# Product-sums of the adaLN modulation, moved in part from VectorE to GpSimd and ScalarE

## Chip, cores and metric

One core of a Trainium2 chip (trn2). The metric is the device time of one execution in microseconds, lower is better. The engines are named as in the profile: PE (TensorE, the matmuls), PEld (its weight loads), DVE (VectorE), ACT (ScalarE), POOL (GpSimd) and SP (SyncE, which here issues nearly all DMAs). Each engine works through its own queue in order; semaphores hold an instruction until its inputs are there and its output tile is free.

## What is computed

A decoder block of 512 positions and 1024 channels, in float32: a state-space mixer and a pooling mixer side by side, merged by gates, and then an MLP. Both halves begin with a norm that is shifted, scaled and gated by a vector `c` (adaLN). All that matters here is the modulation:

```python
mod = (jax.nn.silu(c) @ w_ada[i] + b_ada[i])[:, None, :]
shift_m, scale_m, gate_m, shift_f, scale_f, gate_f = jnp.split(mod, N_MOD, axis=-1)
h = rmsnorm(x, norm_mix_w[i]) * (1.0 + scale_m) + shift_m
x = x + gate_m * hybrid_mixer(h, ...)
h = rmsnorm(x, norm_mlp_w[i]) * (1.0 + scale_f) + shift_f
x = x + gate_f * (jnp.square(jax.nn.relu(h @ w_up[i])) @ w_down[i])
return rmsnorm(x, norm_final_w)
```

`mod` has 6 x 1024 values, each the sum over 1024 products of a row of the transposed `w_ada` with silu(c).

## The kernel before

Channels lie on the 128 partitions, positions on the free axis, so x and h are eight tiles of 128x512. float32 products are made exact enough by splitting each operand into a rounded high part and a low rest (ACT makes the high part, DVE subtracts it) and running three matmuls for each pair. A unit is one 128x1024 block of weights: a DMA into one of four RAW tiles, a cast on ACT (line 144), a subtraction on DVE (line 145), the parts in two of eight HL tiles, and 24 matmuls (lines 154 to 156).

**The modulation.** `mod` is a tile of 128x48; column j is the j-th block of 128 channels (0 to 7 shift, 8 to 15 scale, 16 to 23 gate, 24 to 47 the same for the MLP). `cbc` holds silu(c) on every partition. `ada(j)` loads the j-th 128x1024 block of the transposed `w_ada` (512 KB) and makes the column with one DVE instruction, which multiplies, sums along the free axis and adds the bias (line 170); a very short instruction then reads the sum out.

**The first stage** is written under `manual_schedule`: every engine takes its instructions in the order of the program. After `ada(8)` and `ada(0)`, eight steps k follow. Each loads and splits its starting weights (line 273 on ACT, line 277 on DVE, a 32-column cast on POOL, line 278), makes two columns of `mod` (line 170), the scale on ACT (line 264), the normalised and scaled x on DVE (line 302), its shifted high part on ACT (line 303) and the low part on DVE (line 305), and 18 matmuls over six units of projections (line 315) with two narrow ones for dt (line 309). The tiles of adaT lie in eight EARLY tiles, which are tiles of later stages.

**After it** the order of each engine's queue is set by a scheduler: the program order is the priority, `high_priority` goes ahead of it, and an instruction can be put earlier than its place in the program when its inputs and its tile are free. `issue_after(ins)` holds instructions behind `ins` on its engine. Four groups of the state-space mixer follow (`ssd_group`), with other units between their steps as fillers. Each group uses four 128x1024 tiles m (from three MT tiles) for the decay matrix; the last readers of m are the matmuls of line 520. Beside the fourth group run the pooling units (`pool_in`, with the running sums of line 600, the first of them on POOL and the others on DVE, line 604 and the split of line 125) and `pool_mix`.

Then come three loops of eight units: gates with `wgate[8 + j]`, each with `ada(16 + j)`; the pooling branch with `wbp[j]` and `ada(24 + j)`; the gates of the other branch with `wgate[j]` (lines 696 to 701) and `ada(32 + j)`, held behind the split of that step. The output loop with `wout[j]` has the residual (line 728), its square (line 735) and sum (line 736), and the last eight columns, two in a step from j = 2 on. In all these the tile of adaT is one of the four RAW tiles, which the weights use too. The MLP follows and is not touched.

Of the kernel before, what the change touches and what calls it, by code (L numbers as in the profile page):

```python
# [7 lines left out]
F32 = mybir.dt.float32  # L8
F32R = mybir.dt.float32r
AF = mybir.ActivationFunctionType  # L10
ALU = mybir.AluOpType

P = 128
# [29 lines left out]
class Slots:  # L43
# [13 lines left out]
    def put(self, *ts):  # L57
        for t in ts:
            self.free.append(self.owner.pop(id(t))[0])


def block_kernel(tc, xp, crow, arow, par, adaT, wstart, wz, wx, wpool_in, wgate, wpw, wbs, wbp, wout, wup, wdn, out):
    nc = tc.nc
    act, dve, pool, pe, sp = nc.scalar, nc.vector, nc.gpsimd, nc.tensor, nc.sync

    with (
# [23 lines left out]
        MT = Slots(lambda i, dt: D(NRAW + NHL + i, dt).rearrange("p (h k) -> p h k", h=HG), 3)  # L90
# [7 lines left out]
        def col(name, j=0, n=1, rows=P):  # L98
            a = COLS[name] + j
            return par_t[:rows, a:a + n]  # L100
# [5 lines left out]
        mod = sb.tile([P, 48], F32, name="mod")  # L106
        amod = sb.tile([P, 16], F32, name="amod")
        tri = sb.tile([P, P], F32, name="tri")
        zeros = sb.tile([P, NC], F32, name="zeros")
        ea = sb.tile([P, NH], F32, name="ea")  # L110
        dtk = sb.tile([P, NC, NH], F32, name="dtk")
        ncs = sb.tile([P, NC, NH], F32, name="ncs")
        cd = [sb.tile([P, NC, HG], F32, name=f"cd{i}") for i in range(2)]
        dec = [sb.tile([P, NC, HG], F32, name=f"dec{i}") for i in range(2)]
        cbc = D(NRAW + NHL + 3, F32)
# [3 lines left out]
        done = [None]  # L119
# [46 lines left out]
        def ada(j, at=RAW):  # L166

            r = at.get()
            sp.dma_start(r, adaT[j])
            dve.tensor_tensor_reduce(r, r, cbc, 1.0, col("b_ada", j), ALU.mult, ALU.add, mod[:, j:j + 1])  # L170
            at.put(r)

        def column_sums(ps, sqs, c0, c1, opened=False):

# [41 lines left out]
        EARLY = Slots(lambda i, dt: early[i // 2][:, 2 * (i % 2):2 * (i % 2) + 2, :].rearrange("p a b -> p (a b)"), 8)  # L216
        with tc.manual_schedule():
            raw0 = RAW.get()
            crow_t = raw0[:1]
            act.dma_start(crow_t, crow)  # L220
            mt = [MT.get() for _ in range(3)]
            xs1 = HL.get()
            xpair = [m.rearrange("p h k -> p (h k)") for m in mt] + [xs1]
            xs0 = [xpair[k // 2][:, k % 2 * T:k % 2 * T + T] for k in range(8)]
            for i in range(4):
                sp.dma_start(xpair[i], xp[i])
            sp.dma_start(par_t, par)
            warm(12)
            wide = HL.get()
            dve.memset(wide, 0.0)  # L230
            act.activation(wide[:1], crow_t, AF.Silu)
            cps = [PU.get(), PU.get()]
            for i in range(2):
                pe.matmul(cps[i], ones, wide[:, i * T:(i + 1) * T], start=True, stop=True)
            HL.put(wide)
            ps = PU.get()
            sq = [HL.get() for _ in range(4)]

            def halves(i):
                dve.tensor_tensor(sq[i][:, :T], sq[i][:, :T], sq[i][:, T:], ALU.add)  # L240

            def sums(i):
                pe.matmul(ps, ones, sq[i][:, :T], start=i == 1, stop=i == 3)

            for i in range(3):
                act.activation(sq[i], xpair[i], AF.Square)
                halves(i)
                if i == 1:
                    dve.tensor_tensor(sq[1][:, :T], sq[1][:, :T], sq[0][:, :T], ALU.add)
            act.copy(cbc[:, :T], cps[0])  # L250
            act.activation(sq[3][:, :T], xpair[3][:, :T], AF.Square)
            act.copy(cbc[:, T:], cps[1])
            act.preload_act_table_set("natural_log_exp_and_others")
            dve.tensor_tensor(sq[3][:, T:], xpair[3][:, T:], xpair[3][:, T:], ALU.mult)
            halves(3)
            for i in range(1, 4):
                sums(i)
            warm(5)
            PU.put(*cps)
            RAW.put(raw0)  # L260
            HL.put(*sq)

            def scale(k):
                act.activation(amod[:, k:k + 1], mod[:, 8 + k:9 + k], AF.Identity,
                               bias=col("nmix", k), scale=col("nmix", k))

            W0 = 6 * P + NH

            def begin(k):

                r, hi, lo = RAW.get(), HL.get(F32R), HL.get(F32R)
                sp.dma_start(r[:, :W0], wstart[k])
                act.copy(hi[:, :W0], r[:, :W0])
                return r, hi, lo

            def end(r, hi, lo):
                dve.tensor_tensor(lo[:, :W0], r[:, :W0], hi[:, :W0].bitcast(F32), ALU.subtract)
                pool.tensor_copy(hi[:, W0:W0 + NH], lo[:, W0 - NH:W0].bitcast(F32))
                RAW.put(r)
                HL.put(hi, lo)  # L280
                return [(hi[:, o:o + n], lo[:, o:o + n]) for o, n in [(6 * P, 2 * NH)] + [(o, P) for o in range(0, 6 * P, P)]]

            h = []
            ada(8, EARLY)
            R = S.get()
            act.activation(R, ps, AF.Ln, bias=eps_t, scale=1.0 / DM)
            act.activation(R, R, AF.Exp, scale=-0.5)
            PU.put(ps)
            ada(0, EARLY)
            scale(0)  # L290
            first = [PS.get() for _ in range(8 - NPU)] + [PU.get() for _ in range(NPU - 1)]
            for k in range(8):
                hi, lo = S.get(F32R), S.get(F32R)
                h.append((hi, lo))
                t = S.get()
                shift = mod[:, k:k + 1]
                w = begin(k)
                if k:
                    ada(8 + k, EARLY)
                    scale(k)  # L300
                    ada(k, EARLY)
                dve.scalar_tensor_tensor(t, xs0[k], amod[:, k:k + 1], R, ALU.mult, ALU.mult)
                act.activation(hi, t, AF.Identity, bias=shift)  # L303
                w = end(*w)
                dve.scalar_tensor_tensor(lo, t, shift, hi.bitcast(F32), ALU.add, ALU.subtract)
                S.put(t)
                def dt_unit():
                    for i in range(2):
                        pe.matmul(first[0][:2 * NH], w[0][0], h[k][i], start=k == 0 and i == 0, stop=k == 7 and i == 1)

                for i in range(3):
                    if k == 7 and i == 2:
                        dt_unit()
                    for u in range(1, 7):
                        pe.matmul(first[u], w[u][i // 2], h[k][i % 2], start=k == 0 and i == 0, stop=k == 7 and i == 2)  # L315
                if k < 7:
                    dt_unit()
            sp.dma_start(ea, arow[0:1, :].broadcast_to([P, NH]))
            act.activation(ea, ea, AF.Exp)
# [349 lines left out]
        for j in range(8):  # L669
            gp = F.get()  # L670
            ps = unit(wgate[8 + j], h)
            behind(act.activation(gp, ps, AF.Sigmoid))
            PU.put(ps)
            merged.append(gp)
            if j == 1:
                for _ in rest:
                    pass
                later.append(SZ.get())
                F.free += range(12, 16)
                PU.free += PS.free  # L680
            if j == 3:
                for i in range(4):
                    bs(3, i)()
                pool_mix(1)()
            ada(16 + j)
        for j in range(8):
            ps = unit(wbp[j], pout)
            dve.tensor_tensor(merged[j], merged[j], ps, ALU.mult)
            PU.put(ps)
            ada(24 + j)  # L690
        free(pout)
        mg = []
        for j in range(8):
            gs = F.get()
            ps = unit(wgate[j], h)
            last = act.activation(gs, ps, AF.Sigmoid)
            PU.put(ps)
            dve.tensor_tensor(gs, gs, acc[j], ALU.mult)
            dve.tensor_tensor(gs, gs, merged[j], ALU.add)
            S.put(acc[j])  # L700
            F.put(merged[j])
            mg.append(split(gs))
            F.put(gs)
            with tc.issue_after(done[0].ins):
                ada(32 + j)
        free(h)
        with tc.issue_after(last.ins):
            table = act.preload_act_table_set("natural_log_exp_and_others")
# [42 lines left out]
        for j in range(5):  # L751
            ps = unit(wout[j], mg)
            residual(ps, j, 16)
            PU.put(ps)
            ada(40 + j)
            if j > 1:
                ada(43 + j)
        for k in range(8):
            dve.tensor_scalar(
                amod[:, 8 + k:9 + k], mod[:, 32 + k:33 + k], 1.0, col("nmlp", k), ALU.add, ALU.mult)  # L760
# [405 lines left out]
```

## Time and profile before

| what | value |
|---|---|
| median of 3 runs | 972.45 us (971.51 to 973.26) |
| profiled execution, its own time | 972.32 us |
| span of the profiled execution | 970.6 us |
| busy: PE, DVE, ACT, POOL | 953.3, 658.7, 532.0, 62.8 us |
| product-sums in the first stage, 128x1024 (line 170) | 16, 1.27 to 1.28 us each |
| product-sums later (line 170) | 32, 1.28 us each, from 382.4 to 598.9 us |
| granted clock of PE | 0.996 |

The span runs from the first to the last instruction of the program; the own time has in addition what lies around it. The ends of matmuls are modelled, so that a busy PE isn't a PE at its peak. A row of a timeline has the start, the duration, the engine, the line, the operation, the output and inputs, and in brackets how long the engine had been idle and what ended that. Durations of neighbours on DVE overlap by some 0.07 us; from start to start is what an instruction takes of the queue. "SPq L169" is the issue of a DMA on SP. In a list of instructions of one line stand the shortest, median and longest duration in ns.

### The profile page before, as it was taken

How to read it: one execution, taken by the hardware profiler on the slowest of the kernel's cores; microseconds unless marked ns; L12 is line 12 of the kernel's file. 1: busy time of each engine (PE TensorE's matmuls, PEld its weight loads, DVE VectorE, ACT ScalarE, POOL GpSimd, SP SyncE). 2: the span in 40 equal slices, each digit the busy share in tenths (PEclk: the TensorE clock that was granted, in tenths of full speed). 3: DMA queues.
4: the chain of work that ended last, by engine and by line, in shares of the span. 5: the costliest groups of instructions: out<-in, count | busy, mean ns of one | idle time of the engine just before them, and what ended most of it. 6: DMA issues, size and time to landing. Idle time of an engine off the chain costs nothing.

```text
span 970.6 us, 13204 instructions
## 1 busy us (share of the span) xinstructions
PE 953.3 (98%) x5119; PEld 802.8 (83%) x5119; DVE 658.7 (68%) x965; ACT 532.0 (55%) x830; POOL 62.8 (6%) x71
## 2 busy tenths in 40 slices
PE   8999999999999999999999999999999999999996
PEld 4777778888878878788888878998899889889986
DVE  7996958475776586978533887895557556764633
ACT  6488988579538932562321433684157236425732
POOL 0101120130012012200000000000000000000000
PEclk9999999999999999999999999999999999999998
DMA  9747433442454244327733588441144225204002
GB/s 372 270 142 198 130 99 104 114 126 70 120 142 119 87 120 116 128 88 256 237 87 107 177 279 251 152 153 57 64 138 133 65 70 171 86 35 151 24 1 87
DMA packets 61761, 129.22 MB, mean 133 GB/s; under 512 B 4673, under 2 KB 29377, under 8 KB 61698
## 3 DMA queue, kind: packets, MB, share of 16 engines
q1 hardware_dynamic: 61696, 128.38, 41.5%
q8 instruction: 40, 0.66, 0.3%
q14 instruction: 23, 0.19, 0.1%
q10 hardware_dynamic: 2, 0.00, 0.0%
HBM read 126.13 MB, written 2.23 MB: 132 GB/s over the span
## 4 chain that ended last, share of the span: by engine, by line
PE 88%; DVE 5%; DMA 3%; ACT 2%; issue 1%; POOL 0%; DVEq 0%; SPq 0%; ACTq 0%; POOLq 0%
PE ps L154 22%; PE ps L155 22%; PE ps L156 22%; PE ps L864 12%; PE ps L315 3%; PE ps L520 1%; PE ps L504 1%; PE ps L500 1%; DMA d<-wout 1%; DVE d L170 1%; PE ps L476 1%; DMA d<-adaT 1%; DMA d<-cs_d 1%; DMA d<-wup 0%; DMA d<-xp 0%
## 5 line engine op out<-in xcount | busy, mean ns | idle before, releaser
L154 PE MATMUL ps<-s,d 128*128 128x512 f32 (+1 forms) x1088 | 416.0, 383 | 3.2 <-ACT d L144 1.1
L155 PE MATMUL ps<-s,d 128*128 128x512 f32 (+1 forms) x1088 | 411.7, 379 | 0.0
L156 PE MATMUL ps<-s,d 128*128 128x512 f32 (+1 forms) x1088 | 411.4, 379 | 0.0
L154 PEld LDWEIGHTS ps<-s,d 128*128 128x128 f32 x1088 | 204.3, 188 | 45.4 <-issue 2.4
L156 PEld LDWEIGHTS ps<-s,d 128*128 128x128 f32 x1088 | 204.5, 188 | 38.8 <-DVE d L145 0.3
L155 PEld LDWEIGHTS ps<-s,d 128*128 128x128 f32 x1088 | 204.8, 188 | 37.4 <-DVE s L125 0.2
L144 ACT CAST d<-d 128x1024 fp32r<-128x1024 f32 x89 | 92.8, 1044 | 119.9 <-PE ps L155 99.2
L145 DVE TENSOR_TENSOR d<-d,d 128x1024 fp32r<-128x1024 f32 x89 | 111.1, 1249 | 63.3 <-ACT d L144 62.1
L864 PE MATMUL ps<-s,d 128*128 128x256 f32 x864 | 103.8, 279 | 0.0
L864 PEld LDWEIGHTS ps<-s,d 128*128 128x128 f32 x864 | 102.9, 188 | 0.2
L805 ACT CAST d<-d 128x1024 fp32r<-128x1024 f32 x44 | 45.8, 1050 | 79.2 <-PE ps L155 62.7
L805 ACT CAST d<-sz 128x1024 fp32r<-128x1024 f32 x32 | 33.6, 1051 | 68.9 <-PE ps L155 48.9
L1053 DVE SCALAR_TENSOR_TENSOR xs<-ps,mod,xs 128x512 f32<-128x512 f32 x29 | 21.7, 750 | 69.6 <-PE ps L156 69.6
L806 DVE TENSOR_TENSOR d<-d,d 128x1024 fp32r<-128x1024 f32 x44 | 53.5, 1223 | 21.5 <-ACT d L805 20.1
L806 DVE TENSOR_TENSOR d<-sz,d 128x1024 fp32r<-128x1024 f32 x32 | 39.2, 1224 | 19.7 <-ACT d L805 18.4
L472 ACT ACTIVATE d<-d,ncs 128x128 f32<-128x128 f32 x128 | 41.8, 391 | 11.3 <-POOL d L468 11.1
L170 DVE CUSTOM_DVE_ANT_0 d<-d,d,par_t 128x1024 f32<-128x1024 f32 x32 | 40.8, 1278 | 8.7 <-DMA d<-adaT 8.7
L383 DVE SCALAR_TENSOR_TENSOR s<-ps,par_t,s 128x511 f32<-128x511 f32 (+2 forms) x54 | 40.1, 743 | 1.8 <-ACT s L381 1.4
L315 PE MATMUL ps<-s,d 128*128 128x512 f32 x144 | 35.2, 396 | 2.2 <-ACT s L303 2.2
L315 PEld LDWEIGHTS ps<-s,d 128*128 128x128 f32 x144 | 26.3, 188 | 10.0 <-ACT s L303 4.8
L806 DVE TENSOR_TENSOR s<-pad,s 128x512 fp32r<-128x512 f32 x34 | 23.1, 688 | 7.9 <-ACT s L805 7.7
L468 POOL TENSOR_SCALAR_AFFINE_SELECT d<-d 128x1024 f32<-128x1024 f32 x16 | 19.9, 1244 | 132.6 <-ACT cd L465 59.9
(216 smaller groups left out, 1005.3 us busy)
## 6 DMA issues: line engine op xcount, KB each, us to landing
d<-adaT SPq DMA_DIRECT2D x32, 512.0 KB, 4.3
d<-wx SPq DMA_DIRECT2D x18, 512.0 KB, 3.8
d<-wdn SPq DMA_DIRECT2D x18, 512.0 KB, 3.7
d<-wz SPq DMA_DIRECT2D x16, 512.0 KB, 3.6
d<-cs_d SPq DMA_DIRECT2D x16, 512.0 KB, 6.0
d<-wbs SPq DMA_DIRECT2D x16, 512.0 KB, 3.6
d<-wgate SPq DMA_DIRECT2D x16, 512.0 KB, 3.6
sz<-wdn SPq DMA_DIRECT2D x14, 512.0 KB, 3.8
```

Source lines behind the costliest of these rows:

```text
L144: act.copy(hi[:, :w], r[:, a:a + w])
L145: (low or dve).tensor_tensor(lo[:, :w], r[:, a:a + w], hi[:, :w].bitcast(F32), ALU.subtract)
L154: pe.matmul(ps, whi, xhi[:, t0:t1], start=start, stop=False)
L155: pe.matmul(ps, whi, xlo[:, t0:t1], start=False, stop=False)
L156: pe.matmul(ps, wlo, xhi[:, t0:t1], start=False, stop=stop)
L170: dve.tensor_tensor_reduce(r, r, cbc, 1.0, col("b_ada", j), ALU.mult, ALU.add, mod[:, j:j + 1])
L315: pe.matmul(first[u], w[u][i // 2], h[k][i % 2], start=k == 0 and i == 0, stop=k == 7 and i == 2)
L383: dve.scalar_tensor_tensor(t[:, sh:], ps[:, :T - sh], w(3 - sh), t[:, sh:], ALU.mult, ALU.add)
L472: act.activation(m[:, i, :], m[:, i, :], AF.Exp, bias=ncs[:, c, g * HG + i:g * HG + i + 1])
L805: act.copy(dst[0], src)
L806: dve.tensor_tensor(dst[1], src, dst[0].bitcast(F32), ALU.subtract)
L864: pe.matmul(ps, x, y, start=start and m == 0 and i == 0, stop=m == 3 and i == 2, skip_group_check=True)
```

## The change

A product-sum can now be made in two instructions: `ada_begin` loads the block and multiplies it by `cbc` on POOL, and `ada_end` sums it by a copy on ACT with an accumulated output.

- In the first stage, `ada(8)` and `ada(0)` stay as they were, and so do the shifts `ada(k)`. The scales 9 to 15 go the new way: step k begins the one of step k + 1 (`ahead`), and `end` of step k makes its sum. The bias of the scale is folded, once, into eight columns `shifted`, which the scale's instruction on ACT takes in place of the norm's weight.
- Later, columns 16 and 17 stay on DVE. Columns 18 to 44 go the new way (`ada_later`), and each makes the sum of the one before it. Their tiles are MT tiles instead of RAW tiles. Their bias is added for eight columns at once (`biased`), on DVE. The hold on the third loop's is gone. Columns 45 to 47 stay on DVE.

```diff
+        eb = sb.tile([P, 8], F32, name="eb")
...
             r = at.get()
             sp.dma_start(r, adaT[j])
-            dve.tensor_tensor_reduce(r, r, cbc, 1.0, col("b_ada", j), ALU.mult, ALU.add, mod[:, j:j + 1])
+            dve.tensor_tensor_reduce(r, r, cbc, 1.0, col("b_ada", j) if j < 16 else zeros[:, :1], ALU.mult, ALU.add, mod[:, j:j + 1])
             at.put(r)
+
+        begun = []
+
+        def ada_begin(j, r, put):
+
+            sp.dma_start(r, adaT[j])
+            pool.tensor_tensor(r, r, cbc, ALU.mult)
+            begun.append((j, r, put))
+
+        def ada_end():
+
+            while begun:
+                j, r, put = begun.pop(0)
+                act.activation(r, r, AF.Copy, accum_out=mod[:, j:j + 1])
+                put()
+                if j in (23, 31, 39):
+                    biased(j - 7)
+
+        def biased(j):
+
+            dve.tensor_tensor(mod[:, j:j + 8], mod[:, j:j + 8], col("b_ada", j, 8), ALU.add)
+
+        def ada_later(j):
+
+            ada_end()
+            m = MT.get()
+            ada_begin(j, m.rearrange("p h k -> p (h k)"), lambda: MT.put(m))
...
+            shifted = eb[:, :8]
+            dve.scalar_tensor_tensor(shifted, col("b_ada", 8, 8), 1.0, col("nmix", 0, 8), ALU.add, ALU.mult)
+
             def scale(k):
                 act.activation(amod[:, k:k + 1], mod[:, 8 + k:9 + k], AF.Identity,
-                               bias=col("nmix", k), scale=col("nmix", k))
+                               bias=shifted[:, k:k + 1] if k else col("nmix", k), scale=col("nmix", k))
+
+            def ahead(k):
+                r = EARLY.get()
+                ada_begin(8 + k, r, lambda: EARLY.put(r))
...
                 pool.tensor_copy(hi[:, W0:W0 + NH], lo[:, W0 - NH:W0].bitcast(F32))
+                ada_end()
                 RAW.put(r)
...
                 w = begin(k)
                 if k:
-                    ada(8 + k, EARLY)
                     scale(k)
                     ada(k, EARLY)
+                if k < 7:
+                    ahead(k + 1)
...
-            ada(16 + j)
+            if j < 2:
+                ada(16 + j)
+            else:
+                ada_later(16 + j)
...
-            ada(24 + j)
+            ada_later(24 + j)
...
-            with tc.issue_after(done[0].ins):
-                ada(32 + j)
+            ada_later(32 + j)
...
-            ada(40 + j)
+            ada_later(40 + j)
+            if j == 4:
+                ada_end()
             if j > 1:
                 ada(43 + j)
+        biased(40)
```

## The prediction

> **What bounds the kernel now.** I read the page first, then a table of stretches, then the timeline of the stretches in which the changed lines run.
>
> ```profile
> span 970.6 us, 13204 instructions
> ...
> PE 953.3 (98%) x5119; PEld 802.8 (83%) x5119; DVE 658.7 (68%) x965; ACT 532.0 (55%) x830; POOL 62.8 (6%) x71
> ...
> PE 88%; DVE 5%; DMA 3%; ACT 2%; issue 1%; POOL 0%; DVEq 0%; SPq 0%; ACTq 0%; POOLq 0%
> ```
>
> TensorE ends the time; POOL is almost empty. The profiled execution took 972.32 us (1.7 us around its span), 0.1 us below the median of the runs, so the sum is made against 972.3. Relief for DVE can only pay where TensorE waits, and a delay costs where TensorE has no lead. The stretches (us; then busy time and count of PE, PEld, DVE, ACT, POOL; granted clock; DMA share; GB/s):
>
> ```profile
> 14.60:52.00 37.40, 37.36 (x163) 28.60 (x163) 36.76 (x54) 17.27 (x28) 5.11 (x8) 1.00 0.80 302
> ...
> 376.00:402.00 26.00, 25.29 (x137) 20.11 (x136) 24.58 (x41) 9.67 (x16) 9.51 (x8) 1.00 0.31 102
> 402.00:426.00 24.00, 24.00 (x107) 19.84 (x106) 20.51 (x29) 14.02 (x21) 3.44 (x2) 1.00 0.42 132
> 426.00:476.00 50.00, 50.00 (x222) 41.39 (x221) 39.74 (x56) 24.33 (x31) 0.00 (x0) 1.00 0.66 219
> 476.00:540.00 64.00, 64.00 (x284) 53.01 (x283) 22.42 (x24) 14.08 (x16) 0.00 (x0) 1.00 0.36 109
> ```
>
> Two stretches have DVE full: the first stage (36.76 of 37.40) and the pooling stage (24.58 of 26). From 476 to 540 it is two thirds idle. One step k of the first stage, from its timeline (start, duration, engine, line; in brackets the idle time before):
>
> ```profile
> 28.66 0.74 DVE L305 SCALAR_TENSOR_TENSOR s<-s,mod,s 128x512 fp32r<-128x512 f32 x1
> ...
> 28.81 0.67 POOL L278 CAST d<-d 128x32 fp32r<-128x32 f32 x1 [3.98 <-DVE d L277]
> ...
> 29.32 1.27 DVE L170 CUSTOM_DVE_ANT_0 xs<-xs,d,par_t 128x1024 f32<-128x1024 f32 x1
> ...
> 30.53 1.28 DVE L170 CUSTOM_DVE_ANT_0 xs<-xs,d,par_t 128x1024 f32<-128x1024 f32 x1
> 30.64 0.39 ACT L264 ACTIVATE amod<-mod,par_t 128x1 f32<-128x1 f32 x1 [1.29 <-DVE mod L170]
> ...
> 31.73 0.74 DVE L302 SCALAR_TENSOR_TENSOR s<-d,amod,s 128x512 f32<-128x512 f32 x1
> 32.40 0.98 DVE L277 TENSOR_TENSOR d<-d,d 128x800 fp32r<-128x800 f32 x1
> 32.51 0.72 ACT L303 ACTIVATE s<-s,mod 128x512 fp32r<-128x512 f32 x1 [1.48 <-DVE s L302]
> ...
> 33.14 0.85 ACT L273 CAST d<-d 128x800 fp32r<-128x800 f32 x1
> 33.29 0.30 PEld L315 LDWEIGHTS ps<-s,d 128*128 128x128 f32 x2 [0.30 <-ACT s L303]
> ```
>
> From start to start DVE spends 0.66 on L305, 1.21 and 1.20 on the two product-sums, 0.67 on L302 and 0.90 on L277: 4.64 us with no idle time. TensorE needs almost the same; its weight load waits 0.30 us on L303, mostly under running matmuls. Taking away one product-sum therefore bares TensorE at once, and pays about 0.1 us a step.
>
> **What the product on POOL costs DVE.** The trace has POOL and DVE running two-input operations at once:
>
> ```profile
> 340.40 1.06 POOL L600 TENSOR_TENSOR pad<-pad 128x527 f32<-128x527 f32 x1 [33.56 <-ACT pad L591]
> ```
>
> ```profile
> 340.68 1.87 DVE L145 TENSOR_TENSOR d<-d,d 128x1024 fp32r<-128x1024 f32 x1
> ```
>
> ```profile
> 376.27 1.22 DVE L145 TENSOR_TENSOR d<-d,d 128x1024 fp32r<-128x1024 f32 x1 [4.20 <-ACT d L144]
> ...
> 376.80 1.62 POOL L600 TENSOR_TENSOR pad<-pad 128x527 f32<-128x527 f32 x1 [10.69 <-ACT pad L591]
> ...
> 377.41 1.55 DVE L125 TENSOR_TENSOR s<-s,s 128x512 fp32r<-128x512 f32 x1
> ```
>
> ```profile
> 402.69 0.68 DVE L125 TENSOR_TENSOR s<-s,s 128x512 fp32r<-128x512 f32 x1
> ```
>
> L145 takes 1.22 us alone and 1.87 when it begins behind a running L600: 0.65 longer, just what L600 still had to run (to 341.46), less a start-up. At 376.80 it is the other way round: L600 stands until L145 ends at 377.49, does its 1.0 us, and L125 behind it takes 1.55 instead of 0.68. The two engines take turns, a whole instruction at a time. The cast L278 above shows the same for a SCALAR_TENSOR_TENSOR: 0.67 us for 32 columns, ending 0.08 after L305. Of L170 beside POOL no row exists; it reads two SBUF tiles as L145 does. Its bounds are "as L145" and "not at all"; I take the first.
>
> [...]
>
> The new product's length (128x1024, two inputs) is not in the trace either:
>
> ```profile
> L543 POOL TENSOR_TENSOR s<-s x16: 725/864/1486, 97.9 to 395.6; 128x256 f32<-128x256 f32 x16
> ```
>
> ```profile
> L544 POOL TENSOR_TENSOR s<-s x16: 453/462/1329, 98.7 to 396.7; 128x128 f32<-128x128 f32 x16
> ```
>
> From 128 to 256 columns the shortest grows by 0.27, or 2.1 ns a column, which gives 2.4 us at 1024; in proportion to L600 (1.06 for 527) it is 2.1; by the flat slope from 256 to 527 columns, 1.6. I take 2.1, the largest measured tile scaled, and keep 1.6 to 2.4.
>
> [...]
>
> **The first stage, part by part.** Its marks before, the start of L302 in step 0 and TensorE's start in steps 1 and 7:
>
> ```profile
> 13.08 0.75 DVE L302 SCALAR_TENSOR_TENSOR s<-d,amod,s 128x512 f32<-128x512 f32 x1 [0.45 <-ACT amod L264]
> ...
> 19.37 4.38 PE L315 MATMUL ps<-s,d 128*128 128x512 f32 x18
> ...
> 47.23 2.98 PE L315 MATMUL ps<-s,d 128*128 128x512 f32 x12
> ```
>
> Each step k from 1 loses one L170 (1.21). Each step 0 to 6 gets a product of 2.1 that holds off L305, L277, L302 and L170, which is all of DVE's work there. A step becomes 0.66 + 1.21 + 0.67 + 0.90 + 2.1 + about 0.1 for L278 = 5.64 us, 1.0 longer. In order: L302 of step 0 starts at 13.08 (the 8-column operation added before it, costed as the small memset quoted below, makes 13.2); the first product takes its turn behind L302 or L277, so L305 of step 0 ends at 13.2 + 0.67 + 2.1 + 0.90 + 0.66 = 17.55. TensorE runs out of high parts after 6 matmuls and waits about 1.3. Then L278, L170 (to 18.85), the second product (to 20.95), L302 of step 1, and 1.56 later, as from 31.73 to 33.29, TensorE starts step 1: 22.5 instead of 19.4. Five periods of 5.64 put step 6 at 50.7; step 7 has no product and follows at TensorE's own 4.64: 55.3, against 47.2. **+8.1 us**; with 1.6 it is +4.6, with 2.4 +10.2. If L170 runs beside the product, a step is 4.43, TensorE bounds again, and only the late start stays: +1.7.
>
> What lies beside this: the sum on ACT (nearest row: a Square of 1024 columns, below, 1.06; a readout behind it between 0 and the 0.39 of L264, taken as nothing) makes ACT 0.85 + 0.39 + 0.72 + 1.1 = 3.1 of 5.64. The chain product, sum, L273, L264, L302 has some 1.8 us to spare in step 2. A tile of adaT is asked for before the next step's weights on SP; those (128x800, 0.41 MB at the stretch's 302 GB/s) land 1.4 us later, and their cast now runs three us later anyway. L278 stands behind the product on POOL, but TensorE needs it 4 us after L305. The four 8-column bias additions, of the memset's size, are needed only by the residuals after 576: 0.
>
> ```profile
> 7.02 1.06 ACT L246 ACTIVATE d<-d 128x1024 f32<-128x1024 f32 x1 [0.32 <-DMA d<-xp]
> ```
>
> **The later sums.** Outside the hand-ordered first stage, work is put as early as its inputs and its tile allow:
>
> ```profile
> 2.38 0.12 DVE L590 MEMSET pad<- 128x16 f32 x3
> ```
>
> That is the pooling stage's memset, 340 us ahead. Before, the later product-sums shared the four RAW tiles with the weights and so stayed near their place. The change gives them the three MT tiles, last read by TensorE (L520) at:
>
> ```profile
> 357.30 1.02 PE ps L520 x16
> ```
>
> ```profile
> 377.02 1.09 PE L520 MATMUL ps<-d,s 128*64 128x128 f32 x16
> ...
> 384.60 1.09 PE L520 MATMUL ps<-d,s 128*64 128x128 f32 x16
> ```
>
> ```profile
> d<-adaT SPq DMA_DIRECT2D x32, 512.0 KB, 4.3
> ```
>
> The old hold on the gate's product-sums (behind L125) goes too. So I expect all 27 to run through these tiles from 358 on: 4.3 landing + 0.6 for the turn + 2.1 + 1.1 = 8.1 us a round. That puts 3, 3 and 2 products into 376 to 402, where DVE is full: 17 us of port. About 4 lie beside operations with a PSUM input (L527, L537), 1.4 in idle time; **+11 us** reach the wait that ends there:
>
> ```profile
> 401.60 0.50 PE L154 MATMUL ps<-s,d 128*128 128x512 f32 x1 [0.71 <-ACT s L618]
> ```
>
> Its chain runs back through DVE to the POOL operation at 376.80, so delay there is paid in full. From 402 to 426 some 9 products cost DVE 14 us more, but weights lie ahead: the casts wait for TensorE to free a tile, not the reverse.
>
> ```profile
> 413.95 1.06 ACT L144 CAST d<-d 128x1024 fp32r<-128x1024 f32 x1 [3.39 <-PE ps L155]
> ```
>
> The eight HL tiles hold four units, each 24 matmuls at 4.38/18 = 0.24 us, and cover that; without the cover it costs up to 14. What goes: two waits that product-sums cause now.
>
> ```profile
> 577.88 0.73 PE L154 MATMUL ps<-s,d 128*128 128x512 f32 x2 [0.73 <-ACT s L124]
> ```
>
> ```profile
> 592.29 0.50 PE L154 MATMUL ps<-s,d 128*128 128x512 f32 x1 [1.14 <-ACT d L144]
> ```
>
> The first is behind three L170 in DVE's queue, the second behind a wout load, and loads wait for RAW tiles that L170 holds (from the waits of SP's queue: total, times, longest):
>
> ```profile
> SPq L139 <- DVE mod L170: 18.9, 6, 6.2
> ```
>
> Both go: -1.9; what is late next is the norm behind the residuals, unchanged. Sum: 8.1 + 11 - 1.9 = +17.2, so 972.3 + 17.2 = **989.5 us**.
>
> **Rivals.** *A, as above*, 984 to 1001: 0.52. *B, the later sums stay near their place* (the order is not theirs to change, or POOL's turn comes late): they fall into 426 to 560 where DVE has room, all three waits go, 8.1 - 2.6 = +5.5: 977.8. For it: the memset is one instruction, not a chain over SP, POOL and ACT; against it: nothing holds that chain but three tiles. 0.20. *C, faster: the port does not bite*, L170, L302 and L305 run beside the product (only TENSOR_TENSOR rows are long beyond doubt). Then a step is TensorE's, 0.1 x 7 is won, and the three waits go: -3.3, 969.0. It decides from a held time under 1.2 us a product. Against it: 1.87 and 1.55 above. 0.10. *D, only L170 runs beside*, later sums as B: +1.7 - 2.6, 971.4: 0.08. *E, the delay feeds itself*: sums wait in ACT's queue for late products, with casts and splits behind them, and SP waits for MT tiles with weights behind; the 14 after 402 are paid too, +31 and more: 1003.5 to 1020: 0.10.
>
> **How the numbers follow.** Likeliest 989.5. The range 971.5 to 1008 reaches over A and B, the ends 1.6 and 2.4, and into D and E, leaving out C, half of D and part of E, under 2 in 10. A measurement tells about 0.2% from no change: faster 0.11 (C and a little of D), within it 0.07, slower 0.82.
>
> **What would show it.** Right: first-stage steps of about 5.6 us on TensorE, with DVE operations lengthened by the product's turn; products of 2 us on POOL between 358 and 430; a wait of some 10 us near 400; none at 577 and 592. Wrong: steps of 4.6 (C, D); products from 430 on (B). L170 next to a product, 1.28 or 3.4 us long, settles its lock.

## The result, and the profile after

The changed kernel takes 1021.39 us (median of 6 runs, 1016.41 to 1023.00) against 971.36 us for the kernel before beside it: a ratio of 1.050, 95% interval 1.047 to 1.053, or 50 us more. Forecast were 989.5 us and a range up to 1008: the sign was right, the loss of 17 us that was forecast is a third of what came, and the result lies 13 us above the range. The profiled execution is the fastest of the six, 1016.41 us, and its span is 44.1 us longer than that of before; the trace below accounts for these 44 us.

The page of the changed kernel: span, busy time of each engine, the granted clock in 40 slices, and the shares of the chain that ended last.

```profile
span 1014.7 us, 13257 instructions
...
PE 964.7 (95%) x5119; PEld 808.4 (80%) x5119; DVE 664.9 (66%) x902; ACT 567.2 (56%) x898; POOL 158.1 (16%) x105
...
PEclk9999999999999999697999999999999999999999
...
PE 77%; DVE 9%; DMA 5%; ACT 4%; issue 2%; POOL 2%; SPq 0%; DVEq 0%; POOLq 0%; ACTq 0%
```

VectorE gave up 34 product-sums and is busy for 6 us more, not 43 us less. The chain has left TensorE for 23% of the span, from 12% before, and in two slices the granted clock falls to 0.6 and 0.7. Where that is, the stretches show (columns as before: busy time and count of PE, PEld, DVE, ACT, POOL; clock; DMA share; GB/s):

```profile
400.00:432.00 32.00, 18.11 (x62) 13.87 (x61) 31.24 (x26) 15.23 (x26) 27.49 (x14) 0.73 0.48 161
432.00:458.00 26.00, 26.00 (x116) 21.47 (x115) 24.03 (x19) 11.50 (x20) 18.14 (x8) 1.00 0.54 182
458.00:486.00 28.00, 15.91 (x45) 11.68 (x44) 15.17 (x21) 22.18 (x33) 16.72 (x6) 0.70 0.51 169
...
506.00:600.00 94.00, 94.00 (x416) 77.86 (x415) 38.68 (x43) 31.38 (x40) 0.00 (x0) 1.00 0.33 101
```

Between 400 and 432 TensorE runs 62 matmuls, where it can run some 140 (116 in 26 us in the next stretch, 0.224 us each). VectorE is full there, and GpSimd nearly so. From 506 to 600 TensorE waits for nothing.

**The first stage** came out near the forecast. TensorE's starts of the steps 1, 6 and 7, from its timeline:

```profile
22.66 4.38 PE L352 MATMUL ps<-s,d 128*128 128x512 f32 x18 [0.86 <-ACT s L340]
...
50.49 4.38 PE L352 MATMUL ps<-s,d 128*128 128x512 f32 x18 [0.72 <-ACT s L340]
...
55.17 2.90 PE L352 MATMUL ps<-s,d 128*128 128x512 f32 x12
```

Step 1 starts at 22.66 (forecast 22.5), step 6 at 50.49 (50.7), step 7 at 55.17 (55.3; before 47.23). That is +7.9 us where +8.1 stood. The five periods between are 5.57 us (5.64). VectorE and GpSimd within one of them (lines 171 and 339 are 170 and 302 of the kernel before):

```profile
28.91 1.27 DVE L171 CUSTOM_DVE_ANT_0 sz<-sz,d,par_t 128x1024 f32<-128x1024 f32 x1
29.01 3.42 POOL L179 TENSOR_TENSOR xs<-xs,d 128x1024 f32<-128x1024 f32 x1
...
30.29 2.69 DVE L339 SCALAR_TENSOR_TENSOR s<-d,amod,s 128x512 f32<-128x512 f32 x1
```

They take turns: the product L179 starts during the product-sum, stands until that ends (at about 30.2), and runs to 32.43; L339 starts at 30.29 and ends 0.55 after the product, having taken 2.69 us in place of 0.74.

**The later sums** run early, as forecast. The first product starts at 370.46, beside VectorE operations with one input in PSUM (L515, 0.68 us from 370.61, as elsewhere), and takes 2.40 us; GpSimd's list has all 27 started by 503.5:

```profile
370.46 2.40 POOL L179 TENSOR_TENSOR d<-d,d 128x1024 f32<-128x1024 f32 x1 [11.04 <-DMA d<-adaT]
```

```profile
L179 POOL TENSOR_TENSOR d<-d,d x27: 2346/2522/6451, 370.5 to 503.5; 128x1024 f32<-128x1024 f32 x27
```

What the forecast missed is what follows on TensorE. Its timeline, first instruction behind each wait over 1 us from 370 to 500 (the bracket has the idle time and what ended it):

```profile
393.19 1.16 PE L537 MATMUL ps<-s,s 128*128 128x128 f32 x8 [3.77 <-DVE s L549]
...
415.61 0.79 PE L155 MATMUL ps<-s,d 128*128 128x512 f32 x1 [6.22 <-ACT pad L628]
...
426.21 0.80 PE L155 MATMUL ps<-s,d 128*128 128x512 f32 x1 [7.67 <-ACT pad L628]
...
464.76 0.80 PE L155 MATMUL ps<-s,d 128*128 128x512 f32 x1 [5.21 <-ACT xs L709]
...
466.21 0.63 PE L155 MATMUL ps<-s,d 128*128 128x512 f32 x1
466.63 0.63 PE L156 MATMUL ps<-s,d 128*128 128x512 f32 x1
...
469.74 0.40 PE L155 MATMUL ps<-s,d 128*128 128x512 f32 x1
469.97 0.40 PE L156 MATMUL ps<-s,d 128*128 128x512 f32 x1
...
478.31 0.80 PE L155 MATMUL ps<-s,d 128*128 128x512 f32 x1 [5.66 <-ACT s L125]
480.33 0.79 PE L156 MATMUL ps<-s,d 128*128 128x512 f32 x1 [1.22 <-DVE s L126]
```

The six waits sum to 29.8 us. Four of them end with an instruction of ACT: one that empties a tile of PSUM (`ps`, the output of these matmuls; the copy L628, the sigmoid L709), or the split of an activation (L125). None ends with a weight. And each of these long waits has a tail of slow matmuls: behind the wait of 5.21 us they still start 0.42 us apart at 466.21, and 0.23 again only at 469.74. The granted clock is 0.73 from 400 to 432 and 0.70 from 458 to 486. The stretches of the kernel before, and one of the changed kernel, give the whole:

```profile
370.00:486.00 116.00, 115.28 (x536) 94.72 (x535) 88.49 (x127) 52.01 (x70) 12.95 (x10) 1.00 0.51 166
506.00:600.00 94.00, 92.12 (x404) 75.34 (x404) 62.82 (x92) 28.92 (x38) 0.00 (x0) 1.00 0.60 193
```

```profile
370.00:486.00 116.00, 86.25 (x355) 67.97 (x354) 86.71 (x85) 60.18 (x95) 77.69 (x35) 0.84 0.51 168
```

From 370 to 486 the kernel before ran 536 matmuls, the changed kernel 355. The 181 that are missing are worth 40.5 us at 0.224; TensorE idles for 116 - 86.25 = 29.75 of them, so about 10 us lie in the tails. VectorE runs 85 instructions there in place of 127 and is as busy as before (86.7 us against 88.5): the turns have eaten what the product-sums left. From 506 to 600 the changed kernel is ahead, 416 matmuls to 404: 2.7 us.

Why ACT is late with these, its timeline and VectorE's show, for the waits that end at 393.19 and 415.61:

```profile
387.11 1.06 ACT L186 ACTIVATE d<-d 128x1024 f32<-128x1024 f32 x1 [5.02 <-POOL d L179]
...
409.58 1.06 ACT L186 ACTIVATE d<-d 128x1024 f32<-128x1024 f32 x1 [6.28 <-POOL d L179]
...
414.46 0.63 ACT L579 ACTIVATE s<-sz 128x512 f32<-128x512 f32 x1 [2.80 <-DVE sz L578]
414.99 0.57 ACT L628 COPY pad<-ps 128x512 f32<-128x512 f32 x1
```

```profile
389.23 1.22 DVE L146 TENSOR_TENSOR d<-d,d 128x1024 fp32r<-128x1024 f32 x1 [5.28 <-ACT d L145]
...
399.76 3.43 DVE L171 CUSTOM_DVE_ANT_0 d<-d,d,zeros 128x1024 f32<-128x1024 f32 x1
...
407.47 2.10 DVE L639 TENSOR_TENSOR pad<-pad,par_t 128x16 f32<-128x16 f32 x1
...
411.71 2.71 DVE L578 TENSOR_TENSOR sz<-s,sz 128x512 f32<-128x512 f32 x1
```

Before 415.61 ACT stood 6.28 us with a sum at the head of its queue, whose product was late, and then 2.80 us for L578, which a product held: it lasted 2.71 us. The copy L628 behind them is what TensorE needs. The VectorE operations with two SBUF inputs that begin here behind a running product last longer by about what is left of it: L171 3.43 us in place of 1.28 with 2.35 us left, L578 2.71 (its shortest is 0.68) with 2.17, and L639, 16 columns, 2.10 (its shortest is 0.16) with 2.07.

So ACT stands for two things, late products and held VectorE operations, and the trace has both. Before 393.19 VectorE was not held but idle, 5.28 us, for a weight's cast on ACT; the cast stood behind a sum, the sum 5.02 us for its product, and the product 4.70 us for its load. Before 426.21 ACT stood 3.70 and 1.61 us for products. Before 464.76 it stood 7.46 us for L641, which a product held (2.83 us); two sums, a cast and a load of ACT's function table (1.28 us) then came ahead of L709. Before 478.31 it stood 1.94 us for a product, and two more sums and two table loads followed, with VectorE idle for most of that time; the kernel before has as many table loads. Which of the two costs, the runs have to tell.

### The profile page after: what moved, and what is told of

Same layout as the page of the kernel before. It is cut to its first block, busy times and chain, and to the rows that moved or that the text cites. A ratio compares the mean times of both kernels' runs of the same rounds, so it can differ in the third digit from the quotient of the medians.

```text
span 1014.7 us, 13257 instructions
## 1 busy us (share of the span) xinstructions
PE 964.7 (95%) x5119; PEld 808.4 (80%) x5119; DVE 664.9 (66%) x902; ACT 567.2 (56%) x898; POOL 158.1 (16%) x105
## 4 chain that ended last, share of the span: by engine, by line
PE 77%; DVE 9%; DMA 5%; ACT 4%; issue 2%; POOL 2%; SPq 0%; DVEq 0%; POOLq 0%; ACTq 0%
PE ps L155 20%; PE ps L156 20%; PE ps L157 20%; PE ps L906 12%; DMA d<-adaT 2%; POOL d L179 2%; PE ps L557 1%; DVE d L146 1%; DMA d<-cs_d 1%; DVE pad L637 1%; DVE s L339 1%; DVE s L641 1%; PE ps L541 1%; PE ps L352 1%; ACT d L145 1%
## 5 line engine op out<-in xcount | busy, mean ns | idle before, releaser
L146 DVE TENSOR_TENSOR d<-d,d 128x1024 fp32r<-128x1024 f32 x89 | 114.8, 1291 | 96.2 <-ACT d L145 94.5
L145 ACT CAST d<-d 128x1024 fp32r<-128x1024 f32 x89 | 92.3, 1040 | 67.0 <-PE ps L156 64.2
L179 POOL TENSOR_TENSOR d<-d,d 128x1024 f32<-128x1024 f32 x27 | 73.9, 2745 | 54.0 <-DMA d<-adaT 40.2
L848 DVE TENSOR_TENSOR d<-d,d 128x1024 fp32r<-128x1024 f32 x44 | 53.5, 1224 | 24.2 <-ACT d L847 16.1
L186 ACT ACTIVATE d<-d 128x1024 f32<-128x1024 f32 x27 | 28.5, 1056 | 53.2 <-POOL d L179 53.2
L848 DVE TENSOR_TENSOR d<-sz,d 128x1024 fp32r<-128x1024 f32 x32 | 39.2, 1224 | 19.8 <-ACT d L847 16.5
```

Of the source, the lines that this page charges most:

```text
L145: act.copy(hi[:, :w], r[:, a:a + w])
L146: (low or dve).tensor_tensor(lo[:, :w], r[:, a:a + w], hi[:, :w].bitcast(F32), ALU.subtract)
L179: pool.tensor_tensor(r, r, cbc, ALU.mult)
L848: dve.tensor_tensor(dst[1], src, dst[0].bitcast(F32), ALU.subtract)
```

## The experiments

Two theories stood at first. **The port** (the prediction's word for what VectorE and GpSimd take turns at): a product on GpSimd holds VectorE off, and VectorE's lateness reaches TensorE through ACT's queue. **The queues**: the sums wait in ACT's queue (or other work in GpSimd's) for a product, whatever VectorE does. A third came with the later ones: the sums simply run too early. All later_ kernels are later_only with one more edit, all first_ ones first_only with one. Ratios are against runs of the kernel before beside each; us are the difference of the medians.

| run | edit | ratio (95%) | us |
|---|---|---|---|
| first_only | only the first stage changed | 1.0055 (1.0036 to 1.0075) | +6.2 |
| later_only | only the later sums changed | 1.0399 (1.0343 to 1.0455) | +38.2 |
| later_no_product | no product | 1.0071 (1.0047 to 1.0095) | +7.0 |
| later_no_sum | no sum on ACT | 1.0466 (1.0437 to 1.0494) | +45.3 |
| later_held | loads held behind weights | 1.0261 (1.0242 to 1.0280) | +25.3 |
| later_memset | two memsets for the product | 1.0027 (1.0011 to 1.0044) | +2.6 |
| later_mt_dve | one VectorE instruction, as early | 1.0028 (1.0015 to 1.0041) | +2.1 |
| later_pad_dve | GpSimd's running sum on VectorE | 1.0433 (1.0414 to 1.0451) | +42.4 |
| first_memset | two memsets for the product | 0.9999 (0.9986 to 1.0013) | -0.2 |
| later_half | product over 512 columns | 1.0208 (1.0184 to 1.0232) | +19.2 |
| held_memset | later_held with memsets | 1.0038 (1.0011 to 1.0065) | +2.4 |
| mt_from_32 | see below | 0.9976 (0.9965 to 0.9987) | -2.8 |

**The two parts alone.** first_only takes the hunks of the later loops back, later_only those of the first stage.

```diff
 # first_only
...
-            ada_later(24 + j)
+            ada(24 + j)
...
 # later_only
...
                 if k:
+                    ada(8 + k, EARLY)
...
-                if k < 7:
-                    ahead(k + 1)
```

> The first-stage part alone, the later product-sums as before. The changed kernel's TensorE reaches the end of the first stage 7.9 us later than before (60.1 against 52.3), so if the two parts add up: +7 to +9 us, some 979 us. If the late start is made up in later waits: below +4.

> The later part alone, the first stage as before. If the parts add up: 1021.4 - 8 = 1013 us, +40 to +44. If the first stage's delay shifts the later work into a worse order and is part of the large loss: below +30.

+6.2 and +38.2, both a little less than was expected: some 86% of that loss is in the later sums. Of the 7.9 us that the first stage loses in the trace, about 2 are made good further on: TensorE's wait that ended at 135.81 is shorter in the changed kernel and has no slow tail (the last section has the rows). Together the parts give +44.4, the changed kernel +50.0; the 6 us between are not explained (its profiled execution is +44.1).

**Product or sum.** In later_no_product the multiplication goes, in later_no_sum the sum; there a one-element copy on GpSimd stands in its place.

```diff
 # later_no_product
-            pool.tensor_tensor(r, r, cbc, ALU.mult)
 # later_no_sum
-                act.activation(r, r, AF.Copy, accum_out=mod[:, j:j + 1])
+                pool.tensor_copy(mod[:, j:j + 1], r[:, :1])
```

> As later_only without the product on GpSimd (the sums are then over the loaded block itself, so mod lacks the factor silu(c)). Port theory, what costs is DVE held by the products: all of the loss goes, -3 to +1 us against before. Queue theory, what costs is that sums stand in ScalarE's queue ahead of evictions and casts and wait: the wait shrinks to that for the DMA (4.3 us a load, the products waited 40 us for loads in the changed kernel), +5 to +20 us stay.

> As later_only, but instead of the sum on ScalarE GpSimd copies one element (mod is then not the sum). ScalarE waits for no product; products, port and tiles are as in later_only. Port theory: nearly all of the loss stays, +30 to +44 us. Queue theory: most of the loss goes, +3 to +12 us, what is left being DVE held and the pooling sums behind products in GpSimd's queue.

Without the product 7.0 us of 38.2 are left, without the sum all of it. So the loss hangs on the product, and the 28 us that ACT is busy with sums (27 of 1.06) are not what costs. Neither run fell into the range of the port theory: 7.0 is what the queue theory allowed, 45.3 is just above the port's 44 and far from the queue's 12. The trace of later_no_sum, from TensorE's and ACT's timelines, has a wait of the old size with no sum on ACT:

```profile
406.51 0.80 PE L155 MATMUL ps<-s,d 128*128 128x512 f32 x1 [7.76 <-ACT pad L625]
```

```profile
405.35 0.63 ACT L576 ACTIVATE s<-sz 128x512 f32<-128x512 f32 x1 [11.01 <-DVE sz L575]
```

ACT now stands 11.01 us for VectorE itself, and the copy that TensorE needs (L625 here) comes behind that. That leaves open whether the product costs by holding VectorE or by its own length in front of others on GpSimd and in the chain load, product, sum.

**A product that reads nothing.** Two memsets of 0.955 us write the same tile in the product's place: the same tiles, loads, waits and sums, 1.9 us on GpSimd, and no SBUF input.

```diff
-            pool.tensor_tensor(r, r, cbc, ALU.mult)
+            for _ in range(2):
+                pool.memset(r, 0.0)
```

> As later_only, but the product is replaced by two memsets of the tile, which read nothing, and occupy GpSimd about as long (mod is then the bias alone). Port theory: VectorE is not held by them; the loss falls to that without products, +5 to +12 us. GpSimd-queue theory, the pooling sums on GpSimd stand behind products and are late: most of the loss stays, +25 to +40 us.

+2.6 where the product costs +38.2; even the port theory had left more (+5 to +12), and less is left than without any product (+7.0), which stays unexplained. GpSimd's and VectorE's timelines near the place where the product held L171 for 3.43 us, and GpSimd's group:

```profile
398.70 2.86 POOL L180 MEMSET d<- 128x1024 f32 x3
```

```profile
401.05 1.27 DVE L171 CUSTOM_DVE_ANT_0 d<-d,d,zeros 128x1024 f32<-128x1024 f32 x1
```

```profile
L180 POOL MEMSET d<- 128x1024 f32 x54 | 51.3, 955 | 43.4 <-DMA d<-adaT 37.6 <-ACT s L593 3.5 <-ACT pad L626 0.7
```

L171 begins inside a run of memsets and takes its 1.27 us. The memsets, 27 x 1.9 = 51.3 us against the products' 73.9, are not short enough to explain a loss fourteen times smaller; the next run tests that.

**Length.** The product over half of the columns, 1.64 us on the mean, shorter than the two memsets:

```diff
-            pool.tensor_tensor(r, r, cbc, ALU.mult)
+            pool.tensor_tensor(r[:, :512], r[:, :512], cbc[:, :512], ALU.mult)
```

> As later_only, with the product over 512 of the 1024 columns (the sum is over all; mod then lacks silu(c) on half). Port theory: half the hold, about 1.2 us, and VectorE's idle time takes a larger share of it: +8 to +22 us against before. If the number of turns counts and not their length: +30 us or more.

```profile
L179 POOL TENSOR_TENSOR d<-d,d 128x512 f32<-128x512 f32 x27 | 44.1, 1643 | 45.9 <-DMA d<-adaT 43.5 <-PE ps L534 2.4
```

+19.2, half of the loss for half of the columns, with less time on GpSimd (44.1 us) than the memsets' 51.3 at +2.6. Nor is it the sums' waiting: ACT stood 35.4 us in all for products here, 27.2 for the memsets, and 53.2 for the whole products in the changed kernel. What counts in these runs is that the operation reads, and for how long.

**The same in the first stage.** first_only with the same edit as later_memset.

> As first_only, with the product replaced by two memsets of the tile, which read nothing and take GpSimd 1.9 us (the scales 9 to 15 are then the bias alone). Port theory: steps of 4.6 us on TensorE instead of 5.57; against before -1 to +2 us. Chain theory, what is late is the chain product, sum, cast, scale, normalised x: +4 to +6 us, as first_only.

No loss is left (0.9999). TensorE's steps and the VectorE operation that the product held for 2.69 us, beside GpSimd:

```profile
26.78 4.26 PE L353 MATMUL ps<-s,d 128*128 128x512 f32 x18
31.35 4.26 PE L353 MATMUL ps<-s,d 128*128 128x512 f32 x18
```

```profile
29.33 1.97 POOL L180 MEMSET xs<- 128x1024 f32 x2 [0.60 <-DMA xs<-adaT]
```

```profile
29.97 0.75 DVE L340 SCALAR_TENSOR_TENSOR s<-d,amod,s 128x512 f32<-128x512 f32 x1
```

A step is 4.57 us, TensorE's own time, with the sum on ACT and the longer chain in place. The whole +1.0 us a step was VectorE held by the product (2.69 us in place of 0.75), and the sum on ACT is free there, as the prediction costed it. What stays is the late start: step 7 begins at 49.61 in place of 47.23, and the shorter wait near 135 makes that good. The run also shows what the first stage could have won with a product that holds nothing: nothing measurable, because TensorE bounds the step at once.

**Too early, or GpSimd's own queue?** later_mt_dve makes the later sums in one VectorE instruction, in the MT tiles and without holds, so that they can run early. later_pad_dve takes the pooling stage's running sum (line 637) off the queue that the products stand in.

```diff
 # later_mt_dve
...
-            ada_begin(j, m.rearrange("p h k -> p (h k)"), lambda: MT.put(m))
+            r = m.rearrange("p h k -> p (h k)")
+            sp.dma_start(r, adaT[j])
+            dve.tensor_tensor_reduce(r, r, cbc, 1.0, zeros[:, :1], ALU.mult, ALU.add, mod[:, j:j + 1])
+            MT.put(m)
...
 # later_pad_dve
-                    e_ = dve if w >= 2 else pool
+                    e_ = dve
```

> As later_only, but the product-sum is the one VectorE instruction of before; tiles (MT) and the lost hold are as in the change. If running early alone costs, VectorE being full there: 1.2 us for each of some 20, +10 to +20 us. If the split on two engines is what costs: -3 to +4 us.

> As later_only, with the first running sum of each pooling unit on VectorE too, so that no pooling sum stands behind a product in GpSimd's queue. GpSimd-queue theory: most of the loss goes, below +15 us. Port theory: VectorE gets 0.7 us more for each of eight sums and stays held by products: +30 to +45 us.

The one instruction costs +2.1 us, the two +38.2, though the 27 run as early, from 365 to 468: running early through the MT tiles is not the fault. And taking other work out of GpSimd's queue doesn't help (+42.4).

**Sums kept near their place.** Each load of adaT is held on SP behind its unit's weights, once with products and once with memsets.

```diff
-                sp.dma_start(r[:, :n], src)
+                load[0] = sp.dma_start(r[:, :n], src)
...
-            ada_begin(j, m.rearrange("p h k -> p (h k)"), lambda: MT.put(m))
+            with tc.issue_after(load[0].ins):
+                ada_begin(j, m.rearrange("p h k -> p (h k)"), lambda: MT.put(m))
```

> As later_only, but each late load is kept behind the weight load of its own unit in SP's queue, so that one product comes in every 5.4 us from about 400 on and none earlier. Early-running theory, the loss comes from 20 or so products in the stretch where VectorE is full: the loss goes, -3 to +3 us against before. If the products cost wherever they stand (2.4 us of VectorE for 1.2 saved, 27 times): +15 us or more stay.

> As later_held (one load for each unit, in step with the weights), with the product replaced by two memsets that read nothing (mod is then the bias alone). later_held lost 25 us with no product before 400. Port theory: the loss goes, -2 to +4 us. Queue theory, in later_held the sums stand in ScalarE's queue before casts and gates and wait for late loads: +15 us or more stay.

Later is better (+25.3 against +38.2) but far from the gain of 2.6 us that the prediction's rival B gave the later sums there, though VectorE has room from 476 on. Its largest wait, in the timelines of TensorE, GpSimd and ACT:

```profile
597.35 0.79 PE L155 MATMUL ps<-s,d 128*128 128x512 f32 x1 [9.33 <-ACT s L125]
```

```profile
587.65 2.34 POOL L179 TENSOR_TENSOR d<-d,d 128x1024 f32<-128x1024 f32 x1 [15.32 <-DMA d<-adaT]
```

```profile
590.02 1.06 ACT L186 ACTIVATE d<-d 128x1024 f32<-128x1024 f32 x1 [4.01 <-POOL d L179]
```

Here a queue does cost: the product waits 15.32 us for its held load, the sum 4.01 for the product, and the casts and splits behind it come late. So this run alone doesn't tell port from queue. held_memset has the same holds and loses 2.4 us; but the scheduler orders its queues anew for each kernel, so the pair differs in more than the port, and how the 25 us divide is open.

**A version that beats both.** From later_mt_dve and the stretches of before: the kernel before, with its single VectorE instruction, but the columns 32 to 47 in MT tiles in place of RAW tiles, held only until VectorE leaves the full stage, at the first multiplication of the wbp loop.

```diff
+        def ada_mt(j):
+            m = MT.get()
+            r = m.rearrange("p h k -> p (h k)")
+            sp.dma_start(r, adaT[j])
+            with tc.issue_after(from_here.ins):
+                dve.tensor_tensor_reduce(r, r, cbc, 1.0, col("b_ada", j), ALU.mult, ALU.add, mod[:, j:j + 1])
+            MT.put(m)
...
-            dve.tensor_tensor(merged[j], merged[j], ps, ALU.mult)
+            gated = dve.tensor_tensor(merged[j], merged[j], ps, ALU.mult)
+            if j == 0:
+                from_here = gated
...
-            with tc.issue_after(done[0].ins):
-                ada(32 + j)
+            ada_mt(32 + j)
...
```

> The kernel before, with one change: product-sums 32 to 47 stay one VectorE instruction, but in MT tiles and held only behind the first step of the pooling branch, so that they run from about 470 on, where VectorE is two thirds idle. If the waits at 577 and 592 (0.73 and 1.14 us in the trace of before) come from them: -1 to -2.5 us against before. If those waits have other causes: -0.5 to +1 us.

969.55 us against 972.31, 0.24% less (0.13 to 0.35); the 2.8 us are a little more than was expected. The product-sums run from 492 to 527, where VectorE was two thirds idle, each in its 1.28 us, and TensorE no longer waits near 577 and 592 (stretches, then the list of the line):

```profile
476.00:540.00 64.00, 64.00 (x284) 53.00 (x283) 42.13 (x63) 14.91 (x17) 0.00 (x0) 1.00 0.65 222
540.00:585.00 45.00, 45.00 (x198) 36.82 (x197) 28.74 (x37) 22.13 (x31) 0.00 (x0) 1.00 0.52 173
585.00:600.00 15.00, 15.00 (x68) 12.42 (x67) 5.85 (x7) 4.02 (x6) 0.00 (x0) 1.00 0.25 79
```

```profile
L179 DVE CUSTOM_DVE_ANT_0 d<-d,d,par_t x16: 1275/1284/1285, 491.9 to 526.0; 128x1024 f32<-128x1024 f32 x16
```

## Why the prediction was right, and where it was wrong

- **The port: right.** "I take the first", as L145, was the choice for L170. L171 lasts 3.43 us beside a product and 1.27 beside memsets, which settles what the prediction calls its lock: the product, which reads SBUF, held it, and the memsets, which read nothing, did not. With memsets the loss goes from +6.2 to nothing in the first stage and from +38.2 to +2.6 later.
- **The product's size: 2.40 us, the upper bound, not 2.1.** That alone is small: in the first stage two errors cancelled, the longer product and a step with less around it, and +7.9 came for +8.1. That this is so near is luck; by the prediction's own sum 2.40 would have given +10.2.
- **The wait by 402: near in size, by luck.** +11 us were forecast, from eight products between 376 and 402 that hold VectorE. Five start there, not eight: most of them wait for their loads. The forecast took off 4 us for operations with a PSUM input; the prediction shows no row for that. The trace of the changed kernel has two of the kind, L515 with 0.68 us at 370.61 and L564 with 0.33 at 407.21, beside a product and no longer than elsewhere. By 416 TensorE had waited 3.77 + 6.22 = 10.0 us, but the first of these waits came with VectorE idle behind ACT, and 6.28 us of what led to the second were a sum's wait for its product: the path of rival E, which the forecast priced at nothing.
- **The step that failed: "weights lie ahead: the casts wait for TensorE to free a tile, not the reverse".** With it, 14 us from 402 to 426 were costed at nothing. Weights were indeed ahead; no wait after 402 ends with one. The step guarded the wrong resource. TensorE also needs its PSUM tiles emptied (waits of 6.22, 7.67 and 5.21 us end with L628 and L709) and its activations split (5.66 us, L125). These stand in ACT's queue, behind sums that wait for products and behind instructions that wait for held VectorE operations. After the one at 415.61, waits of 7.67, 5.21, 5.66 and 1.22 us follow, 19.8 in all, against the 14 that the prediction named as the most it could cost without the cover; products go on to 506, not to 426. That the product's reading is what makes ACT late, the runs show (+2.6 with memsets, +45.3 without sums); how each single wait divides between the two kinds of standing is open.
- **A term that was left out: the clock.** Each of these long waits is followed by matmuls at about half speed (starts 0.43 us apart for 0.23, a granted clock of 0.73 from 400 to 432 and of 0.70 from 458 to 486), some 10 us in all.
- **The gains: half of them.** The wait at 592 is gone. The one at 577 is not: the first matmuls of the output loop stand at 625.73, again behind a split of ACT (L125), and wait 1.03 us in place of 0.73, with no product-sum on VectorE in the 7 us before it. By idle time 0.8 us remain of 1.9.
- **Together:** 7.9 + 40.5 from 370 to 486, less about 2 near 133 and 2.7 from 506 to 600, is the 44 us of the trace. Of the rivals, E (a chance of 0.10) had the nearest price, 1003.5 to 1020, and half of the mechanism: the delay does pass through ACT's queue, and sums do wait there. But their waiting is not what costs, since without them the loss is as large.

## What to carry to other kernels

When VectorE is full, moving an elementwise operation with two inputs to GpSimd can lengthen VectorE's work: here operations of VectorE became some 2 us longer (L339 2.69 us for 0.74) for 1.2 us saved, and 5% of the time was lost. Before a delay on an engine is costed at nothing, list every resource through which the bounding engine depends on it (inputs, weights, and the copies that free its outputs), and the queue each stands in; cover by one of them is no cover. Here an instruction that was short and in the way was better moved in time, by a tile that let it run where its engine was idle (-2.8 us), than moved to another engine (+50).

## What the runs showed of the hardware

- A small operation paid for all that was left of a product: L639, 16 columns wide, took 2.10 us at 407.47, with 2.07 us of one to run, and 0.17 at 462.98, where no product ran. What it paid went by the product, not by its own size.
- Memsets on GpSimd ran beside VectorE's two-input operations without delay to either: 955 ns on the mean of 54 in later_memset, with L171 at its 1.27 us.
- TensorE's granted clock fell after a wait of 2.22 us. In the kernel before, that much idle time was followed by eight starts 0.43 us apart (a clock of 0.57 from 136 to 140); in the changed kernel (second block) 1.46 us at the same place were not (1.00 from 143 to 147):

```profile
135.81 0.58 PE L555 MATMUL ps<-s,ones 128*128 128x512 f32 x1 [2.22 <-ACT s L124]
136.18 0.63 PE L154 MATMUL ps<-s,d 128*128 128x512 f32 x1
136.61 0.63 PE L155 MATMUL ps<-s,d 128*128 128x512 f32 x1
```

```profile
142.83 0.50 PE L592 MATMUL ps<-s,ones 128*128 128x512 f32 x1 [1.46 <-ACT s L125]
143.17 0.40 PE L155 MATMUL ps<-s,d 128*128 128x512 f32 x1
143.41 0.40 PE L156 MATMUL ps<-s,d 128*128 128x512 f32 x1
```

The rate is about half (0.43 us for 0.23). Why 2.22 us of idle time had this tail and 1.46 had none is open.

- Product and sum as separate instructions cost some 3.6 us of two engines (2.40 on GpSimd, 1.06 and a readout of 0.19 on ACT) for what VectorE does in 1.28.
